# Attention branch's gate as Strassen-Winograd products behind the pooled branch, and weight sums by accumulating DMA, in a two-layer hybrid attention block

## The chip, the cores and the metric

One core of one Trainium2 chip runs the whole program. The metric is the device time in microseconds of one execution, lower is better. TensorE (PE) does the matrix products, VectorE (DVE), ScalarE (ACT) and GpSimd (POOL) the elementwise work, and DMAs are issued by SyncE (SP) and POOL.

## What is computed

Two layers run over T = 528 tokens (16 meta tokens and 512 of the input) of width 1024. In each layer, cut to what matters here:

```python
h = rms_norm(x, g)
q, k, v, gate_a, u_b, gate_b, q_idx, k_idx, w_idx, merge = split(h @ w_in)
attn = indexer_sparse_attention(...)      # 8 heads, top 128 keys by an indexer's score
y_a = (attn * silu(gate_a)) @ w_a         # gate_a: 512 columns of w_in, from column 640
y_b = (multiscale_pool(u_b) * silu(gate_b)) @ w_b
g_a, g_b = split(sigmoid(merge))          # merge: 2048 columns of w_in
x = x + (g_a * y_a + g_b * y_b) @ w_out
```

The result is float32. Each float32 product is three products of fp32r operands: high by high, high by low and low by high part (low = value minus its rounded copy).

## The kernel before

**Weights.** Every weight matrix is cut into chunks of 1 MB (`chunks`, L112). SP loads a chunk into two tiles `raw` (four buffers, so two chunks at a time), and a short list of steps then makes its high and low parts (`w`). `group_done` (L335) takes one step from the front of that list, `prep_q`, after a group of matmuls. There are three kinds of chunk. The ordinary kind (L188 onwards) has ACT round and DVE subtract. A chunk in `by_dma` (L202, L203, L207) has ACT write the negated rounded weights, an accumulating DMA from POOL's queue add the raw ones, and ACT round again. A chunk in `mixed` (`mixed_prep`, L227) makes seven operands out of four quarter blocks for seven products.

**Seven products instead of eight.** The merge gate's eight chunks go through `mix_gates` (L939): a chunk's 1024 by 256 weights and the activations are split into two by two blocks, and each gate (one chunk, q = 0 to 7) is seven block products (a11, a12, s2, s1, s3, s4, a22 in this order) of 12 matmuls each, 264 tokens wide in layer 0 and 256 in layer 1. Of the weights it needs four sums: s3 = a11 - a21, s2 = a22 - s3, s1 = a21 + a22, s4 = a12 - s2, all four made by DVE (`mix`, in steps i1, i2 and i4). Of a chunk's nine steps i0 to i8, each takes some high parts (ACT, L237) and low parts (DVE). The loop in `end` takes steps ahead of need: LEAD = 5 of the nine steps of the next gate are taken before that gate begins. The sums of the activations (`sums_of_h`, L867) are made while the pooled branch's gate and inputs are computed, some go out to DRAM and come back (`far`, `hsheet`), and from then on half of the normalized activations is overwritten by a sum, so no ordinary product of them may follow.

**Order of a layer.** Index queries and keys; gate_b (`silb`); the pooled branch's inputs u, with the pooling on POOL; `queries(0)` (half of the heads); gate_a as two `by_dma` chunks through `dense` (L547: 24 matmuls for one block of 128 columns and one stretch of tokens), with tanh on ACT (L1206) and a product on DVE into `sila`; `queries(1)`; then the product with w_b (16 blocks of 12 matmuls in layer 0, 8 wider ones in layer 1, `zb`, L1237); the eight gates; the product with w_a; the output.

**What runs beside it.** PE and DVE execute in the order in which the program text emits instructions (`manual_schedule`). Two streams are woven in. `fill` holds generators: first the indexer's scores (`index_steps`), then `attention` (L715), which is advanced by half of `rate[0]` turns per `half_done` (L329; a group_done counts as one). A head pair u (16 of them, in a loop of 18 rounds of three turns) goes through logits (PE), minimum (DVE), exp (ACT, L749), scaling (ACT, L760; POOL and DVE `pm`, L761), transposes (PE), copies (ACT, L776) and values (PE). Four head pairs share one block of 128 queries, and `gated(i)` (L802) multiplies a block's result into `sila`. In layer 0 six more turns treat the meta tokens. `attend` is put into `fill` before the product with w_b, at R_ATT = 1.95 and 1.7 for the two layers.

`sel` holds the top-k steps (`topk_steps`, L693): 16 rounds of MAX8 and MATCH_REPLACE8 on the scores, for two pairs of query blocks. `group_done` spends on them what an account has left: FULL times the estimated PE time since the last group, less the estimated DVE time (`pe_cost`, `dve_cost`, L81), at most CAP = 1.5 us. `ensure(i)` (L1213), called at the first logits of a query block, takes all steps that are still missing at once: the first pair's for blocks 0 and 1, the second pair's at block 2 (u = 8).

**Tiles.** `sheet` gives small tiles from six buffers ("tt") or wide ones from six buffers ("L", shared by the softmax rows `lt`, the sum s2 and others). All "d" products rotate through three PSUM banks.

Of the kernel before, what the change touches and what calls it, by code (L numbers as in the profile page):

```python
# [16 lines left out]
KT = D // 128  # L17
# [13 lines left out]
R_ATT = (1.95, 1.7)  # L31
FULL = 1.0
# [48 lines left out]
def dve_cost(name, out, a=None, *rest):  # L81
    if name == "memset":
        return 0.1
    n = max(cols(out), cols(a))
    return 0.15 + n * (0.00052 if name in ("tensor_copy", "tensor_scalar") else 0.00104)
# [3 lines left out]
def tile_block(ctx: ExitStack, tc: tile.TileContext, x, meta, w_in, pool_w, w_a, w_b, w_out, rows, hgain, c_tab, out):  # L89
# [24 lines left out]
    metas = {7: 0, 10: 1}  # L114
    for l in range(2):
        wi = w_rows(w_in[l], 0, w_in.shape[2])

        chunks.append([(wi[:, :, 2176:2432], 0)])
        plain.add(len(chunks))
        chunks.append([(wi[:, :, 512:640], 0), (wi[:, :, 2688:2816], 128)])  # L120
        mb = [3784, 4040, 4296, 4552]
        order = [2432, 1664, 1920, 1408, 1152, 0, 640, 896, 256]
        chunks += [[(wi[:, :, c:c + 256], 0)] for c in order]
        chunks += [[(w_rows(w_b[l], c, 512), 0)] for c in (0, 512)]
        by_dma |= set(range(len(chunks) - 10, len(chunks)))
        mixed |= set(range(len(chunks), len(chunks) + 8))
# [7 lines left out]
    def w_place():  # L134
        c = W["load"]
        W["load"] += 1
        kt = chunks[c][0][0].shape[1]
        raws[c] = [wpool.tile([128, kt // 2, 2048 // kt], F32, tag="raw", name="raw", bufs=4) for s in range(2)]
        return c

    def w_fetch(c, s):
        kt = chunks[c][0][0].shape[1]
        for src, o in chunks[c]:
            nc.sync.dma_start(raws[c][s][:, :, o:o + src.shape[2]], src[:, s * kt // 2:(s + 1) * kt // 2, :])
# [82 lines left out]
    def mixed_prep(c):  # L227

        r0, r1 = raws[c]
        blk = {"a11": r0[:, :, 0:128], "a21": r0[:, :, 128:256], "a12": r1[:, :, 0:128], "a22": r1[:, :, 128:256]}  # L230
        src = {"a11": "a11", "a12": "a12", "a22": "a22", "s3": "a11", "s2": "s2", "s1": "a21", "s4": "a12"}
# [10 lines left out]
        def mix(eng, to, x, y, op):  # L242
            eng.tensor_tensor(blk[to], blk[x], blk[y], op=op)

        def i0():
            hi("a11")

        def i1():
            lo("a11")
            mix(dve, "a11", "a11", "a21", OP.subtract)  # L250
            hi("a12")

        def i2():
            lo("a12")
            blk["s2"] = tmp.tile([128, 544], F32, tag="L", name="s2", bufs=LB)[:, :512].rearrange(
                "p (k e) -> p k e", k=4)
            mix(dve, "s2", "a22", "a11", OP.subtract)
            mix(dve, "a21", "a21", "a22", OP.add)
# [4 lines left out]
        def i4():  # L263
            lo("s2")
            mix(dve, "a12", "a12", "s2", OP.subtract)
# [449 lines left out]
    def attention(ensure):  # L715
# [92 lines left out]
        for u in range(-1, 17):  # L808
            if u + 1 < 16:
# [57 lines left out]
    def sums_of_h(l, s0, n2):  # L867
# [7 lines left out]
        def sums(g):  # L875
            k = slice(2 * g, 2 * g + 2)
            a0, a1, b0, b1 = nf[0][:, k, c0], nf[0][:, k, c1], nf[1][:, k, c0], nf[1][:, k, c1]
            dve.tensor_tensor(a0, a1, a0, op=OP.subtract)
            dve.tensor_tensor(a1, b1, a1, op=OP.subtract)
            dve.tensor_tensor(b1, b1, a0, op=OP.subtract)  # L880
# [4 lines left out]
        def lows(g):  # L885
            k = slice(2 * g, 2 * g + 2)
            a1, b0, b1 = nf[0][:, k, c1], nf[1][:, k, c0], nf[1][:, k, c1]
            dve.tensor_tensor(b0, b0, b1, op=OP.subtract)
# [6 lines left out]
        def fetch(w, g):  # L895
            if (w, g) == (0, 1):
                back[w, g] = [(slice(k, k + 1), sheet(n2, "hsheet")[:, None, :n2]) for k in (2, 3)]
            else:
                t = tmp.tile([128, T], F32, tag="B", name="hsheet", bufs=8) if w == 0 else sheet(T, "hsheet")
# [39 lines left out]
    def mix_gates(zb, ta, s0, n2, operands, splits, alos):  # L939
        base = popped[0] - progress[W["use"]]  # L940
        for q in range(8):
# [5 lines left out]
            U, S, X = (bs[r] for r in ROLES[q % 3])  # L947
# [11 lines left out]
            def end():  # L959
                done[0] += 1  # L960
                group_done()
                while prep_q and (popped[0] < base + 9 * q + LEAD + done[0] * 9 // 7 or (q == 7 and done[0] > 4)):
                    prep_one()

            def gate(eh, t, src, in_sheet):
                j = 2 * q + eh
                cs = slice(s0 + t * n2, s0 + (t + 1) * n2)
                if q < 4:
                    th = src if in_sheet else sheet(n2, "th")[:, :n2]
                    act.activation(th, src, AF.Tanh, scale=0.5)  # L970
                    d = zb[:, j, cs]
                    later(lambda: dve.scalar_tensor_tensor(d, th, 1.0, d, op0=OP.add, op1=OP.mult), 2)
                else:
                    act.activation(ta[j - KT][:, cs], src, AF.Tanh, scale=0.5)

            def total(eh, t, ps, part):
                o = sheet(n2, "c")[:, :n2]
# [35 lines left out]
            ready.pop(c)  # L1013

# [48 lines left out]
    for l in range(2):  # L1063
# [132 lines left out]
        queries(0)  # L1196
        sa = one.tile([128, 4, T], F32, tag="D", name="sila")
        SIL["a"] = sa
        for c in range(2):
            w = chunk()  # L1200
            for mi in range(2):
                j = 2 * c + mi
                for hf, a, n, o in halves:
                    ps = dense(w, mi, a, n)
                    th = sheet(n, "th")
                    act.activation(th[:, :n], ps[:, :n], AF.Tanh, scale=0.5)  # L1206
                    later(lambda th=th, ps=ps, j=j, a=a, n=n: dve.scalar_tensor_tensor(
                        sa[:, j, a:a + n], th[:, :n], 1.0, ps[:, :n], op0=OP.add, op1=OP.mult), 1)
                    group_done()
        queries(1)  # L1210
# [13 lines left out]
        fill.append(attend())  # L1224
        rate[0] = R_ATT[l]
# [16 lines left out]
        last_sum()  # L1242
        ahi = one.tile([128, 4, T], F32R, tag="Ahi", name="ahi")
# [14 lines left out]
        mix_gates(zb, ta, s0, n2, operands, splits, alos)  # L1258
# [154 lines left out]
```

## Time and profile before

| | |
|---|---|
| median of 3 runs | 757.07 us (756.95 to 758.25) |
| profiled execution | 756.37 us, of which its span is 754.6 us |
| granted PE clock | 1.00 |
| instructions | 15640 |
| DMA | 96.94 MB, 128 GB/s on average |
| accumulating DMAs of weights (POOL) | 40 of 512 KB |

A row of groups in the profile reads: line, engine, operation, tiles out<-in, shape, count, then busy time in us, mean ns of one, and the idle time of the engine ahead of it. L61 is a helper's line through which all of PE's and DVE's instructions go, so these are told by their tiles. The chain of work that ended last is printed in pieces that follow each other without overlap: start, duration, what.

### The profile page before, as it was taken

What the parts mean: (1) busy time and instruction counts of PE and PEld (TensorE: products, weight loads), DVE (VectorE), ACT (ScalarE), POOL (GpSimd) and SP (SyncE); (2) the same over time, 40 slices, a digit from 0 to 9 for tenths busy, and PEclk for the clock granted to TensorE, in tenths of its full rate; (3) what the DMA queues carried; (4) which work ended last, traced back from release to release, by engine and by line L of the source; (5) the groups of instructions that cost most, each with busy time, mean ns of one, the idle gap of its engine ahead of it and who ended that gap; (6) DMA issues with size and microseconds to landing.
All of it is one profiled execution on the core that took longest, in us unless ns stands there. A gap on an engine that the chain in (4) does not pass through costs nothing.

```text
span 754.6 us, 15640 instructions
## 1 busy us (share of the span) xinstructions
PE 739.7 (98%) x5914; PEld 707.6 (94%) x5914; DVE 563.7 (75%) x1416; ACT 471.8 (63%) x1049; POOL 213.8 (28%) x280
## 2 busy tenths in 40 slices
PE   8999999999989999999999999999999999999998
PEld 7999999999989999999999989988989899999998
DVE  6866987889798775894358668787998888678531
ACT  7679645558869795543245786555677788764320
POOL 3741075242012100063256401741501011005100
PEclk9999999999999999999999999999999999999999
DMA  7677757775122223543422787667812322146411
GB/s 263 226 167 173 166 127 179 158 200 139 31 82 57 57 57 96 184 143 127 128 87 83 171 190 186 157 151 203 208 38 61 98 67 56 57 135 204 140 43 43
DMA packets 73547, 96.94 MB, mean 128 GB/s; under 512 B 3664, under 2 KB 58736, under 8 KB 73472
## 3 DMA queue, kind: packets, MB, share of 16 engines
q1 hardware_dynamic: 67632, 74.89, 31.9%
q0 software_dynamic: 5760, 20.97, 14.8%
q8 instruction: 46, 0.75, 0.4%
q14 instruction: 29, 0.24, 0.1%
q10 hardware_dynamic: 80, 0.08, 0.0%
HBM read 66.41 MB, written 8.55 MB: 99 GB/s over the span
## 4 chain that ended last, share of the span: by engine, by line
PE 81%; DVE 9%; ACT 6%; issue 1%; POOL 1%; DMA 1%; SPq 0%; DVEq 0%; ACTq 0%
PE d L61 69%; PE a L61 10%; PE v L61 3%; DVE w L61 3%; ACT lt L749 2%; ACT w L237 1%; ACT lt L760 1%; DVE raw L61 1%; DVE lt L61 1%; ACT pt L776 1%; DVE c L61 1%; DVE s L61 1%; DVE sc L61 1%; DVE alo L61 1%; DMA xt<-in_x_dram 1%
## 5 line engine op out<-in xcount | busy, mean ns | idle before, releaser
L61 PE MATMUL d<-hhi,w 128*128 128x256 f32 (+3 forms) x1408 | 287.6, 296 | 0.3 <-DVE c L61 0.2
L61 PEld LDWEIGHTS d<-hhi,w 128*128 128x128 f32 x1408 | 225.9, 188 | 6.0 <-DVE c L61 0.7
L61 PE MATMUL d<-hlo,w 128*128 128x256 f32 (+3 forms) x704 | 193.5, 294 | 0.0
L61 PEld LDWEIGHTS d<-hlo,w 128*128 128x128 f32 x704 | 132.5, 188 | 2.6 <-issue 0.2
L61 PE MATMUL d<-w,hhi 128*128 128x256 f32 x768 | 121.0, 287 | 0.5 <-DVE w L61 0.5
L61 DVE TENSOR_TENSOR w<-raw,w 128x512 fp32r<-128x512 f32 (+1 forms) x128 | 107.7, 851 | 2.4 <-ACT w L237 2.3
L61 PEld LDWEIGHTS d<-w,hhi 128*128 128x128 f32 x768 | 104.3, 188 | 5.0 <-issue 2.1
L761 POOL TENSOR_SCALAR pm<-lt,rs 128x16 f32<-128x16 f32 x48 | 27.8, 592 | 173.3 <-DVE rs L61 166.4
L61 PE MATMUL d<-hsum,w 128*128 128x264 f32 (+1 forms) x576 | 76.6, 286 | 0.0
L61 PEld LDWEIGHTS d<-hsum,w 128*128 128x128 f32 x576 | 71.7, 188 | 0.7 <-ACT lt L760 0.3
L61 PE MATMUL d<-w,hlo 128*128 128x256 f32 x384 | 72.3, 281 | 0.0
L203 POOL DMA_DIRECT2D w<-raw x40 | 36.6, 929 | 104.4 <-ACT w L202 82.6
L237 ACT CAST w<-raw 128x512 fp32r<-128x512 f32 x96 | 56.9, 624 | 2.1 <-DVE raw L61 2.0
L61 PEld LDWEIGHTS d<-w,hlo 128*128 128x128 f32 x384 | 57.0, 188 | 0.0
L1274 POOL TENSOR_TENSOR hlo<-ta,hhi 128x256 fp32r<-128x256 f32 (+1 forms) x28 | 28.2, 1019 | 96.5 <-PE d L61 83.2
L61 DVE MATCH_REPLACE8 sc<-m,sc 128x400 f32<-128x400 f32 (+2 forms) x100 | 54.3, 548 | 0.0
L61 DVE MAX8 m<-sc 128x8 f32<-128x400 f32 (+2 forms) x100 | 52.7, 556 | 0.8
L749 ACT ACTIVATE lt<-lt,mn,NR 128x144 f32<-128x144 f32 (+3 forms) x64 | 42.4, 666 | 13.9 <-DVE mn L61 13.9
L61 PE MATMUL d<-mhi,w 128*128 128x272 f32 (+2 forms) x192 | 47.7, 328 | 0.0
L202 ACT ACTIVATE w<-raw 128x1024 fp32r<-128x1024 f32 x40 | 41.4, 1057 | 8.3 <-PE d L61 8.3
L61 DVE SCALAR_TENSOR_TENSOR sc<-r,wsg,sc 128x144 f32<-128x144 f32 (+3 forms) x56 | 32.3, 580 | 16.2 <-ACT r L673 14.1
L207 ACT CAST w<-raw 128x1024 fp32r<-128x1024 f32 x40 | 41.5, 1050 | 0.0
(209 smaller groups left out, 1391.2 us busy)
## 6 DMA issues: line engine op xcount, KB each, us to landing
raw<-in_w_in_dram SPq DMA_DIRECT2D x72, 512.0 KB, 4.1
w<-raw POOLq DMA_DIRECT2D x40, 512.0 KB, 5.3
raw<-in_w_out_dram SPq DMA_DIRECT2D x16, 512.0 KB, 3.4
kept<-res SPq DMA_DIRECT2D x16, 264.0 KB, 4.0
res<-kept SPq DMA_DIRECT2D x16, 264.0 KB, 5.8
raw<-in_w_branch_b_dram SPq DMA_DIRECT2D x8, 512.0 KB, 3.8
raw<-in_w_branch_a_dram SPq DMA_DIRECT2D x8, 512.0 KB, 3.7
xt<-in_x_dram SPq DMA_DIRECT2D x4, 512.0 KB, 5.6
```

Of the source, the lines that this page charges most:

```text
L61: return fn(*a, **k)
L202: act.activation(t, raws[c][s], AF.Copy, scale=-1.0)
L203: gp.dma_start(t, raws[c][s], accum_op=OP.add)
L207: act.copy(t, raws[c][s])
L237: act.copy(t[:, 0], blk[src[n]])
L749: act.activation(L[hh][:, :n], L[hh][:, :n], AF.Exp, scale=NR[:, i, h:h + 1], bias=mn[:, hh:hh + 1], accum_out=sm[:, hh:hh + 1])
L760: act.activation(L[hh][:, 16:n], L[hh][:, 16:n], AF.Copy, scale=rs[:, hh:hh + 1])
L761: (gp if j < 3 else dve).tensor_scalar(pms[i][:, 2 * j + hh, :], L[hh][:, 0:16], rs[:, hh:hh + 1], None, op0=OP.mult)
L776: act.copy(pt[:, :2 * len(bs)], tp[:, :256 * len(bs)].rearrange("p (a c) -> p a c", c=128))
L1274: pool_end = gp.tensor_sub(hlo[:, j, a:a + n], d, f(hhi[:, j, a:a + n]))
```

## The change

- gate_a's two chunks (columns 640 and 896) move behind the pooled branch's chunks, become `mixed`, and run through `mix_gates` as q = -2 and -1, ahead of the merge gate's eight. `queries(1)` follows `queries(0)` directly.
- `sila` is then written by these two gates. `attend` enters `fill` after the product with w_b, and `attention` yields without work at u = 4 until four groups after gate -1 has ended (`SIL["ready"]`).
- The sums of weights become s3 = a11 + a21, s2 = s3 + a22, s1 = a21 + a22, s4 = a12 + s2. DVE makes s3 and s2, and an accumulating DMA from POOL's queue makes s1 and s4. Signs move into the sums of activations, and into tanh's scale.
- A mixed chunk's quarter blocks are contiguous in `raw`; it is loaded by four DMAs of 256 KB instead of two of 512 KB.
- R_ATT becomes (1.75, 1.6), FULL 1.05, and `dve_cost` a smaller fixed part.
- The returned sum `hsheet` (0, 0) takes a wide "L" tile instead of a "B" tile.

The diff, cut to its core:

```diff
-R_ATT = (1.95, 1.7)
-FULL = 1.0
+R_ATT = (1.75, 1.6)
+FULL = 1.05
...
-    return 0.15 + n * (0.00052 if name in ("tensor_copy", "tensor_scalar") else 0.00104)
+    each = 0.00052 if name in ("tensor_copy", "tensor_scalar") else 0.00104
+    return {"match_replace": 0.13, "tensor_tensor_reduce": 0.18}.get(name, 0.07) + n * each
...
-        order = [2432, 1664, 1920, 1408, 1152, 0, 640, 896, 256]
+        order = [2432, 1664, 1920, 1408, 1152, 0, 256]
...
-        chunks += [[(wi[:, :, c:c + 256], 0)] for c in (*mb, 2760, 3016, 3272, 3528)]
+        chunks += [[(wi[:, :, c:c + 256], 0)] for c in (640, 896, *mb, 2760, 3016, 3272, 3528)]
...
+            for eh in range(2):
+                nc.sync.dma_start(raws[c][s][:, eh], src[:, 4 * s:4 * s + 4, eh * 128:eh * 128 + 128])
...
         def i0():
+            blk["s3"] = tmp.tile([128, 544], F32, tag="L", name="s3", bufs=LB)[:, :512].rearrange(
+                "p (k e) -> p k e", k=4)
+            dve.tensor_add(blk["s3"], blk["a11"], blk["a21"])
+            gp.dma_start(blk["a21"], blk["a22"], accum_op=OP.add)
             hi("a11")
         def i1():
             lo("a11")
-            mix(dve, "a11", "a11", "a21", OP.subtract)
+            dve.tensor_add(blk["a11"], blk["s3"], blk["a22"])
             hi("a12")
         def i2():
             lo("a12")
-            blk["s2"] = tmp.tile([128, 544], F32, tag="L", name="s2", bufs=LB)[:, :512].rearrange(
-                "p (k e) -> p k e", k=4)
-            mix(dve, "s2", "a22", "a11", OP.subtract)
-            mix(dve, "a21", "a21", "a22", OP.add)
+            gp.dma_start(blk["a12"], blk["a11"], accum_op=OP.add)
...
         def i4():
             lo("s2")
-            mix(dve, "a12", "a12", "s2", OP.subtract)
             hi("s1")
...
         for u in range(-1, 17):
+            while u == 4 and not SIL["ready"]:
+                yield
...
-        for q in range(8):
+        for q in range(-2, 8):
...
+                sign = -1.0 if eh else 1.0
+                if q < 0:
+                    th = sheet(n2, "th")[:, :n2]
+                    act.activation(th, src, AF.Tanh, scale=0.5)
+                    d = sa[:, j + 4, cs]
+                    later(lambda: dve.scalar_tensor_tensor(d, th, sign, src, op0=OP.add, op1=OP.mult),
+                          3 if in_sheet else 2)
...
+            if q == -1:
+                later(lambda: SIL.update(ready=True), 4)
...
         queries(0)
+        queries(1)
         sa = one.tile([128, 4, T], F32, tag="D", name="sila")
-        for c in range(2):
-            w = chunk()
-            for mi in range(2):
-                j = 2 * c + mi
-                for hf, a, n, o in halves:
-                    ps = dense(w, mi, a, n)
...
-        queries(1)
...
-        fill.append(attend())
-        rate[0] = R_ATT[l]
...
         last_sum()
+        fill.append(attend())
+        rate[0] = R_ATT[l]
```

More of the change, by code (lines that the diff above doesn't have):

```diff
@@ L137, in w_place @@
         kt = chunks[c][0][0].shape[1]
-        raws[c] = [wpool.tile([128, kt // 2, 2048 // kt], F32, tag="raw", name="raw", bufs=4) for s in range(2)]
+        shape = [128, 2, 4, 128] if c in mixed else [128, kt // 2, 2048 // kt]
+        raws[c] = [wpool.tile(shape, F32, tag="raw", name="raw", bufs=4) for s in range(2)]
         return c
```

49 lines of the change are left out of this document (23 added, 26 removed).

## The prediction

> **What bounds the kernel now.** The page's head comes first, then its first and second part, for the engine that is never free and for its clock.
>
> ```profile
> span 754.6 us, 15640 instructions
> PE 739.7 (98%) x5914; PEld 707.6 (94%) x5914; DVE 563.7 (75%) x1416; ACT 471.8 (63%) x1049; POOL 213.8 (28%) x280
> PEclk9999999999999999999999999999999999999999
> ```
>
> PE is busy in 739.7 of 754.6 us at the full granted clock, so the time is the sum of the matmuls plus 14.9 us in which PE stands. What a change is worth is the matmul time that it takes away plus what it does to those 14.9 us. Where they lie, the windows by stage tell: gate_a in layer 0, the product with w_b, then three windows of the eight gates, and the same gates in layer 1 (columns: length; busy time and count of PE, PEld, DVE, ACT, POOL; clock; DMA share; GB/s).
>
> ```profile
> 128.70:153.90 25.20, 25.20 (x213) 25.00 (x210) 22.04 (x60) 15.45 (x28) 8.78 (x10) 1.00 0.57 126
> 167.30:196.30 29.00, 29.00 (x246) 28.84 (x245) 26.10 (x86) 24.86 (x70) 7.96 (x15) 1.00 0.41 108
> 196.30:230.00 33.70, 31.73 (x279) 30.70 (x278) 31.15 (x85) 25.09 (x63) 4.05 (x6) 1.00 0.23 64
> 230.00:270.00 40.00, 38.88 (x336) 37.50 (x335) 31.77 (x90) 34.51 (x82) 5.35 (x8) 1.00 0.21 55
> 270.00:311.00 41.00, 40.42 (x363) 39.17 (x363) 28.47 (x62) 27.53 (x65) 0.98 (x2) 1.00 0.29 87
> 566.00:600.00 34.00, 32.95 (x285) 31.76 (x286) 29.11 (x81) 27.29 (x70) 4.03 (x6) 1.00 0.25 65
> 600.00:640.00 40.00, 39.47 (x354) 38.05 (x351) 32.88 (x89) 32.78 (x78) 6.22 (x9) 1.00 0.27 78
> 640.00:678.00 38.00, 37.25 (x340) 35.88 (x339) 27.23 (x63) 27.39 (x60) 2.32 (x4) 1.00 0.27 86
> ```
>
> Up to the gates PE never stands. In the gates it stands 1.97 + 1.12 + 0.58 = 3.7 us in layer 0 and 1.05 + 0.53 + 0.75 = 2.3 us in layer 1, 6.0 us together; the rest lies in stages that the change leaves alone. The waits of each gate stage and DVE's order of time say what most of the 6.0 us is.
>
> ```profile
> PEld a L61 <- ACT lt L760: 2.8, 3, 2.1
> ```
>
> ```profile
> 217.41 1.18 DVE L61 MAX8 m<-sc 128x8 f32<-128x400 f32 x2
> 219.11 0.69 DVE L61 MATCH_REPLACE8 sc<-m,sc 128x528 f32<-128x528 f32 x1
> 219.72 0.70 DVE L61 TENSOR_SCALAR sc<-sc 128x400 f32<-128x400 f32 x2
> ```
>
> ```profile
> 591.57 1.85 DVE sc L61 x4
> ```
>
> ```profile
> PEld a L61 <- ACT lt L760: 2.1, 4, 1.1
> ```
>
> Here `ensure` takes the rest of the second pair's top-k at once, a whole round (2.3 us from the first MAX8 to the TENSOR_SCALAR) and the ends, 3.0 us of DVE in these rows. The reciprocal behind it is late, then ACT's scaling, then PE's transposes: the one wait of 2.1 us. In layer 1 the piece of 1.85 us in the chain, from 591.57, does the same, for 1.1 us. So 3.2 of the 6.0 us are forced top-k; 2.8 us are short waits of the attention.
>
> **The change part by part.**
>
> *Columns of matmul (the main term).* In the chain of work, whose pieces follow each other without overlap, a gate_a block of 24 matmuls takes this in layer 0 at 272 and at 256 columns, and one in layer 1 at 512; behind them stand two long stretches of the gates, at 264 and 256 columns.
>
> ```profile
> 129.00 3.06 PE d L61 x24
> 132.93 2.90 PE d L61 x24
> 502.38 2.86 PE d L61 x12
> 297.23 13.36 PE d L61 x108
> 666.46 8.71 PE d L61 x72
> ```
>
> The piece of 2.86 us has only 12 matmuls, half a block, so layer 1's four blocks are eight such pieces. Before: 4 x (3.06 + 2.90) = 23.8 us and 8 x 2.86 = 22.9 us. After, two gates of 84 matmuls in each layer: 168 x 13.36/108 = 20.8 us and 168 x 8.71/72 = 20.3 us. The difference is 3.0 + 2.6 = **-5.6 us**, the eighth that seven products save, less a little since short matmuls cost more for each column. PE has no cover here and nothing to wait for in gate_a now, so all of it counts.
>
> *Work of DVE and ACT.* The rows of one low part, one sum, one high part, one total and gate_a's product (one row of its source line stands for its tanh):
>
> ```profile
> L61 DVE TENSOR_TENSOR w<-raw,w 128x512 fp32r<-128x512 f32 x96 | 64.8, 683 | 2.4 <-ACT w L237 2.3
> L61 DVE TENSOR_TENSOR raw<-raw 128x512 f32<-128x512 f32 x32 | 22.0, 687 | 0.6
> L237 ACT CAST w<-raw 128x512 fp32r<-128x512 f32 x96 | 56.9, 624 | 2.1 <-DVE raw L61 2.0
> L61 DVE TENSOR_TENSOR c<-d,p 128x264 f32<-128x264 f32 x16 | 6.8, 428 | 10.3 <-PE d L61 6.9 <-ACT lt L749 1.8 <-ACT lt L760 1.5
> L1206 ACT ACTIVATE th<-d x12: 374/398/598, 133.0 to 526.0; 128x272 f32<-128x272 f32 x4, 128x256 f32<-128x256 f32 x4, 128x512 f32<-128x512 f32 x4
> ```
>
> A chunk costs DVE 11 x 0.68 us before and 9 x 0.68 after. In layer 0 the gates' windows hold 91.4 us of DVE in 114.7. After: less 8 x 2 x 0.68 = 10.9, plus two chunks 12.3, plus 14 totals and gates at 0.43 = 6.0, plus the five rounds of attention that now lie beside w_b (about 7 us, my estimate from that window's 26.1 less top-k), less the 4 us of top-k left: about 102 us in 114.7 + 20.8 = 135.5 us, 75% instead of 80%. ACT gets 14 x 0.62 + 14 x 0.4 + about 8 = 22 us on 87.1, so 81% instead of 76%. Both stay beside PE: cost 0, between -2.8 us (all short waits go) and +2 (they grow with ACT's share). The changed sums of activations keep their count and sizes; 0.
>
> *Top-k.* DVE's groups in the 26 us ahead of w_b and in w_b's own window, two MAX8 to a round:
>
> ```profile
> L61 DVE MAX8 m<-sc 128x8 f32<-128x528 f32 (+1 forms) x13 | 7.8, 634 | 0.0
> ```
>
> ```profile
> L61 DVE MAX8 m<-sc 128x8 f32<-128x400 f32 (+1 forms) x12 | 7.0, 628 | 0.0
> ```
>
> w_b now comes 25 us earlier, so some 14 rounds instead of 7 are open at its start, at 2.3 us of DVE each. But w_b's window loses the attention, about 19 of its 23 us of DVE become free, and the new account takes more: two MAX8 of 400 and 528 columns took 1.18 us, the old formula puts 1.27, the new one 1.11, and FULL adds 5%. DVE was 22.04 of 25.20 in gate_a's window, and the slack of 12% there and ahead goes to top-k. By u = 8, four gates on, I expect little left to force. Of 3.2 us I take **-2.5** (0 to -3.2). A denser DVE can also be late for PE in the query stages, where q_post reads PSUM: I take **+0.5**, between 0 and 4, the one credit of 1.5 us and 5% of some 50 us.
>
> *Two sums by DMA.* The nearest rows are the accumulating DMAs of twice the size, and the loads with the new short rows beside the old ones.
>
> ```profile
> L203 POOL DMA_DIRECT2D w<-raw x40: 849/874/1218, 43.6 to 540.0; - x40
> DMA to landing us min/median/max: 4.4/5.3/9.4
> raw<-in_w_in_dram SPq DMA_DIRECT2D x72, 512.0 KB, 4.1
> raw<-in_w_in_dram SPq DMA_DIRECT2D x8, 256.0 KB, 4.6
> ```
>
> POOL issues 72 in place of 40, at 0.87 us: 28 us on an engine that is busy in 10.4 of 114.7 us of the gates. Behind a DMA that waits for DVE only `pm` is queued, and its readers come at the end of a query block. The additions are awaited by ACT: s1 is issued in i0 and rounded in i4, s4 issued in i2 and rounded in i6, each time three products apart. A gate lasts 114.7/8 = 14.3 us, so three products are 6.1 us. A landing of 5.3 us after issue fits, with 0.8 us for DVE's lag and for a `pm` ahead of it. If it is late, ACT stands in the cast with exps and copies queued behind it, and PE waits for those. I take **+1.0**, from 0 to 11 (below). [...] The loads: 4.6 instead of 4.1 us, a gate ahead of use and twice as many issues on SP, which PE never awaits; 0.
>
> *Attention's end.* A product gives half of R_ATT: 0.875 and 0.8 turns instead of 0.975 and 0.85. Attention needs 18 x 3 turns, 60 with the meta tokens: 60/0.875 = 69 of the 70 products in layer 0, 54/0.8 = 68 in layer 1. SIL is ready at product 18, when 15.75 and 14.4 turns have been given and 15 are used before u = 4, so hardly a turn is wasted. But now the last `gated`, its split and low part come right ahead of w_a. Before, in layer 0, they ended some ten products earlier:
>
> ```profile
> L61 PE MATMUL v<-pt,VM x4: 217/241/265, 296.9 to 297.0; 16*64 16x64 f32 x4
> ```
>
> ```profile
> L61 PE MATMUL d<-ahi,w x256: 277/281/384, 315.2 to 701.6; 128*128 128x256 f32 x96, 128*128 128x272 f32 x32
> ```
>
> The meta tokens' values, the last of the attention, stand at 297 us, and w_a begins at 315. DVE 0.68, ACT 0.62, DVE 0.69 us in a row, most of it under the last two products and the first block of w_a: **+1.0** for both layers (0 to 5).
>
> Sum: -5.6 - 2.5 + 0.5 + 1.0 + 1.0 = -5.6 us. The profiled execution took 756.37 us, 1.8 around its span and 0.7 below the median of the runs: 750.8, as a median **751.5 us**.
>
> **The rivals.**
>
> *Late additions (slower).* If the DMAs land at 7.4 us, halfway from 5.3 to 9.4, each cast waits 1.2 us: 40 x 1.2 = 48 us of ACT standing. With a quarter of that on PE, 12 us in place of the 1.0: 762. For it: ACT at 81%, POOL in order, 9.4 seen. Against: half the bytes, DMA share of 0.21 to 0.29 in the gates. It decides from (5.6 + 1.0)/40 = 0.17 us of PE wait for each DMA on. [...]
>
> *Attention comes late.* Turns that find DVE or ACT behind push its end past the last gate, into `drain`, where PE has nothing else: at the upper 5 us in place of 1.0, and the forced top-k kept whole, 751.5 + 4 + 2.5 = 758.0, about no change; half of it, 754.8.
>
> *All waits go.* With the 2.8 us of short waits and 3.2 of top-k gone, and no new ones: 757.1 - 5.6 - 6.0 = 745.5; half way 748.
>
> *The columns don't shrink.* If boundaries between short products ate the gain, 757. The two stretches quoted are whole products with their boundaries; hardly.
>
> **How the numbers follow.** The forecast (748.5 to 755.5) gets 0.56, fewer waits 0.13, late attention 0.15, late additions 0.15, no shrinking 0.01. A measurement of this kernel can tell about 0.2%, 1.5 us. Faster: 0.56 + 0.13 + half of late attention = 0.76; same: 0.08; slower: late additions and a rest, 0.16. The range runs from 746.5, which leaves 0.03 below, to 758.5, with the late additions above.
>
> **What would show it.** Right: 168 instead of 192 and 96 matmuls on gate_a's weights, PE's busy time down by 5 to 6 us; no wait of 2 us ahead of the transposes of u = 8, MAX8 ended before them; casts L237 with little idle time behind DMA `raw`; the meta tokens' matmuls just ahead of w_a. Wrong: ACT's casts waiting for the additions, above 0.5 us each; PE idle before w_a by several us; new waits in the queries and in w_b for DVE.

## The result and the profile after

The changed kernel takes **764.17 us** (median of 5 runs, 762.57 to 765.64) beside 758.25 us for the kernel before (5 runs, 756.95 to 758.96). The ratio is **1.008**, 95% interval 1.0057 to 1.0102: slower by 0.8%, where 751.5 us was forecast. Every ratio below is to the kernel before as it ran beside the kernel named, with its 95% interval in brackets; 0.01 is 7.6 us. The profiled execution of the kernel after took 762.6 us.

The head of the page and its row of engines:

```profile
span 760.7 us, 15982 instructions
PE 738.2 (97%) x5962; PEld 708.9 (93%) x5962; DVE 569.7 (75%) x1436; ACT 474.9 (62%) x1077; POOL 238.4 (31%) x312
```

PE is busy for 1.5 us less than before instead of 5 to 6, and it stands for 22.5 us instead of 14.9. The windows by stage say where: in layer 0 the end of the queries, w_b (145.0 to 170.6) and the ten gates; in layer 1 w_b (520.0 to 543.4) and the first gates. The columns are those of the prediction's table.

```profile
130.00:145.00 15.00, 14.73 (x132) 13.52 (x125) 14.32 (x42) 10.04 (x22) 10.04 (x12) 1.00 0.89 213
145.00:170.60 25.60, 25.47 (x213) 25.14 (x212) 25.50 (x65) 15.77 (x37) 8.09 (x9) 1.00 0.55 135
170.60:210.00 39.40, 35.83 (x293) 34.21 (x292) 35.52 (x104) 26.90 (x75) 6.05 (x12) 1.00 0.46 107
210.00:250.00 40.00, 36.40 (x303) 34.92 (x302) 30.43 (x86) 31.30 (x78) 9.50 (x14) 1.00 0.45 103
250.00:290.00 40.00, 38.64 (x354) 37.67 (x355) 26.86 (x77) 32.48 (x76) 7.97 (x13) 1.00 0.46 110
290.00:320.20 30.20, 29.66 (x264) 28.64 (x260) 20.43 (x46) 20.53 (x46) 2.56 (x3) 1.00 0.44 115
520.00:543.40 23.40, 23.40 (x112) 19.02 (x111) 23.30 (x60) 13.21 (x24) 6.51 (x8) 1.00 0.55 128
543.40:580.00 36.60, 33.61 (x261) 32.47 (x260) 33.09 (x96) 24.80 (x69) 6.59 (x11) 0.95 0.47 109
```

Two things are new. DVE has hardly any time free from 130 us to the end of w_b (14.32 of 15.00, 25.50 of 25.60, and 23.30 of 23.40 in layer 1), where the prediction counted on DVE time becoming free. And in the gates PE stands for 3.57 + 3.60 + 1.36 + 0.54 = 9.1 us in layer 0 (3.7 before) and for 3.0 us in the first stretch of layer 1's gates, with the clock at 0.95 there. The waits between 140 and 320 us name the second half of the story.

```profile
ACT w L244 <- DMA raw<-raw: 11.4, 10, 3.7
PEld d L61 <- ACT p L997: 4.9, 3, 3.0
PE d L61 <- ACT p L997: 4.3, 3, 2.8
PE d L61 <- DVE w L61: 1.5, 1, 1.5
```

ACT's rounding of s1 and s4 (L244) stands ten times for the accumulating DMA, up to 3.7 us at once. `p` (L997) is ACT's copy of a product out of PSUM, which is queued behind that rounding, and PE's next product waits for it. The timeline shows one such case, row by row (in brackets the idle time ahead of it and its releaser; `s` is the sum s3):

```profile
230.42 2.19 ACT L244 CAST w<-raw 128x512 fp32r<-128x512 f32 x4 [0.62 <-DMA raw<-raw]
...
236.16 0.67 DVE L61 TENSOR_TENSOR s<-raw 128x512 f32<-128x512 f32 x1
236.23 13.04 SPq L148 DMA_DIRECT2D raw<-in_w_in_dram  x4
...
236.44 1.44 POOL L765 TENSOR_SCALAR pm<-lt,rs 128x16 f32<-128x16 f32 x2 [8.42 <-DVE rs L61]
...
237.82 0.89 POOL L253 DMA_DIRECT2D raw<-raw  x1
...
242.83 0.62 ACT L244 CAST w<-raw 128x512 fp32r<-128x512 f32 x1 [3.68 <-DMA raw<-raw]
...
246.04 0.28 PE L61 MATMUL d<-hhi,w 128*128 128x264 f32 x1
...
248.66 0.38 ACT L997 COPY p<-d 128x264 f32<-128x264 f32 x1
...
249.09 1.52 PEld L61 LDWEIGHTS d<-hsum,w 128*128 128x128 f32 x12 [2.98 <-ACT p L997]
```

The third of the four casts in the first row rounds a11, in step i0, at 231.4. DVE makes s3, of the same step, only at 236.16, and POOL issues s1's addition behind that and behind a `pm`, at 237.82. ACT is at the cast of s1 by 239.15, 1.3 us after the issue. The addition lands at 242.80, 4.98 us after the issue. ACT has lost 3.68 us by then and comes to `p` only at 248.66, and PE stands for 2.8 us behind its matmul of 246.04. The group of all 40 additions shows neither the late issue nor the late landing, because its median is 3.2 us:

```profile
raw<-raw POOLq DMA_DIRECT2D x40, 256.0 KB, 3.2
```

### The profile page after: what moved, and what is told of

The parts are those of the page before. It is cut to its first block, busy times and chain, and to the rows that moved or that the text cites. A ratio compares the mean times of both kernels' runs of the same rounds, so it can differ in the third digit from the quotient of the medians.

```text
span 760.7 us, 15982 instructions
## 1 busy us (share of the span) xinstructions
PE 738.2 (97%) x5962; PEld 708.9 (93%) x5962; DVE 569.7 (75%) x1436; ACT 474.9 (62%) x1077; POOL 238.4 (31%) x312
## 4 chain that ended last, share of the span: by engine, by line
PE 62%; DVE 19%; ACT 9%; DMA 6%; issue 3%; POOL 1%; DVEq 0%; SPq 0%; ACTq 0%; POOLq 0%
PE d L61 52%; PE a L61 8%; DMA raw<-raw 5%; DVE sc L61 4%; DVE m L61 3%; DVE w L61 3%; ACT w L244 3%; ACT lt L753 2%; DVE t L61 2%; PE v L61 2%; DVE qs L61 1%; ACT lt L764 1%; DVE ss L61 1%; DMA xt<-in_x_dram 1%; ACT pt L780 1%
## 5 line engine op out<-in xcount | busy, mean ns | idle before, releaser
L61 PE MATMUL d<-hhi,w 128*128 128x256 f32 (+3 forms) x1344 | 268.8, 292 | 0.5 <-DVE sila L61 0.3
L61 PEld LDWEIGHTS d<-hhi,w 128*128 128x128 f32 x1344 | 214.8, 189 | 3.8 <-issue 0.6
L61 PE MATMUL d<-hlo,w 128*128 128x256 f32 (+3 forms) x672 | 183.2, 289 | 0.0
L61 DVE TENSOR_TENSOR w<-raw,w 128x512 fp32r<-128x512 f32 (+1 forms) x152 | 124.5, 829 | 4.0 <-ACT w L244 3.9
L61 PE MATMUL d<-hsum,w 128*128 128x264 f32 (+1 forms) x720 | 98.5, 289 | 7.8 <-ACT p L997 4.5
L61 PEld LDWEIGHTS d<-hsum,w 128*128 128x128 f32 x720 | 91.0, 191 | 10.4 <-ACT p L997 5.7
L244 ACT CAST w<-raw 128x512 fp32r<-128x512 f32 x120 | 70.8, 620 | 40.8 <-DVE raw L61 20.9
L210 POOL DMA_DIRECT2D w<-raw x32 | 29.5, 940 | 72.5 <-ACT w L209 50.0
L61 DVE SCALAR_TENSOR_TENSOR sc<-r,wsg,sc 128x144 f32<-128x144 f32 (+3 forms) x56 | 32.3, 581 | 16.1 <-ACT r L677 13.6
L253 POOL DMA_DIRECT2D raw<-raw x20 | 17.8, 889 | 79.3 <-DVE s L61 74.9
L640 POOL TENSOR_TENSOR t<-t,t 128x256 f32<-128x256 f32 (+1 forms) x34 | 30.8, 907 | 26.8 <-DVE t L61 26.5
```

The costliest lines, as they stand in the source:

```text
L61: return fn(*a, **k)
L210: gp.dma_start(t, raws[c][s], accum_op=OP.add)
L244: act.copy(t[:, 0], blk[src[n]])
L253: gp.dma_start(blk["a21"], blk["a22"], accum_op=OP.add)
L640: gp.tensor_tensor(t1[:m, :256], t1[:m, :256], t2[:m, :256], op=OP.add)
```

## The experiments

Theory 1 at the start: the additions by DMA land too late for ACT. Theory 2: DVE, crowded by top-k behind w_b, is late for PE. Rivals: the attention's place and rates; the new account; the seven products do not shrink gate_a.

### Who pays: the two sums

**a_dve_sums**: the kernel after, s1 and s4 added by DVE.

```diff
         def i0():
...
-            gp.dma_start(blk["a21"], blk["a22"], accum_op=OP.add)
...
         def i2():
             lo("a12")
-            gp.dma_start(blk["a12"], blk["a11"], accum_op=OP.add)
+            dve.tensor_add(blk["a21"], blk["a21"], blk["a22"])
...
         def i4():
             lo("s2")
+            dve.tensor_add(blk["a12"], blk["a12"], blk["a11"])
```

> The changed kernel with s1 and s4 added by DVE (two additions of 0.68 us more for each of 20 chunks, none by DMA). Theory 1, late additions: ACT's casts no longer wait for a DMA (19.3 us in 17 waits in the changed kernel), so neither does PE for ACT's copy p (about 5 us of PE in layer 0); the time falls by about 5 us against the changed kernel, to about 759. Theory 2, top-k too dense: DVE is full from 130 to 210 us anyway and gets 27 us more work, so the time stays near 764 or rises by 1 to 3.

Measured: 755.2 us, 0.9974 [0.9963, 0.9986], better than theory 1 expected. The additions by DMA cost 1.06 points, **8 us**, more than DVE's 40 extra additions do.

**e_late_casts**: the additions stay with the DMA, but the results are rounded one step later (s1 in i5, s4 in i7; s3 and a22 go ahead; NEEDS 6 and 8).

```diff
         def i4():
             lo("s2")
-            hi("s1")
+            hi("s3")
         def i5():
-            lo("s1")
-            hi("s3")
+            lo("s3")
+            hi("s1")
...
```

> The changed kernel with the same work, but the casts of s1 and s4 come one step later (s3 and a22 are rounded first), about 1.6 us more from addition to cast. Theory 1: most of the 17 waits of ACT for a DMA (mean 1.1 us) go, and PE's waits for p and the exps with them: about 760. Theory 2: PE's waits come from DVE's backlog, and it stays at 764 within 1 us.

Measured: 757.58 us, 1.0002 [0.9992, 1.0013]: 0.78 points, 6 us, from the order of the casts alone. ACT now stands for the additions 10 times for 9.3 us in all, instead of 17 times for 19.3.

**i_s4_by_dma**: s1 by DVE (in i4), s4 by DMA, both rounded late as in e.

```diff
         def i0():
...
-            gp.dma_start(blk["a21"], blk["a22"], accum_op=OP.add)
...
         def i4():
             lo("s2")
-            hi("s1")
+            dve.tensor_add(blk["a21"], blk["a21"], blk["a22"])
+            hi("s3")
...
```

> The changed kernel with s1 by DVE, s4 alone by DMA, and with the later casts. Of the 17 waits of ACT for a DMA 11 were for s1, the long ones among them, and those that remain with the later casts were 6. Theory 1: no wait over 1 us remains, DVE saves 0.68 us a chunk against sums all by DVE: 753.5 to 755.5. If any addition by DMA costs (POOL's issue, the DMA engines), 756 or more.

Measured: 753.9 us, 0.9958 [0.9943, 0.9973], 0.44 points under e. So with the late casts it is s1's addition by DMA that costs, and s4's costs nothing that shows beside a; 11 of the 17 casts that stood in the kernel after were s1's.

### The account, and the attention's rates

**b_old_account** is the kernel after with FULL = 1.0 and the old `dve_cost`; **c_sums_account** is b with a's sums.

```diff
-FULL = 1.05
+FULL = 1.0
...
-        return 0.08
+        return 0.1
...
-    return {"match_replace": 0.13, "tensor_tensor_reduce": 0.18}.get(name, 0.07) + n * each
+    return 0.15 + n * each
```

> The changed kernel with FULL = 1.0 and the old dve_cost, so that top-k is spread as thinly as before. Theory 2, top-k too dense: DVE is no longer full ahead of the first gates, its additions and low parts are on time there, and the waits of the first 40 us of gates (3.6 us of PE in layer 0, 3.0 in layer 1, and a dip of the clock of 1.7 us) go: about 759. Theory 1, late additions: the waits at 187, 246 and 260 us stay, and more top-k is forced at u = 8 (2 to 3 us for each layer): 763 to 768.

> The changed kernel with s1 and s4 added by DVE and the old account of top-k: of the change only gate_a as fourteen products, the new sums' signs and the rates are left. If theories 1 and 2 each hold a part, this is the fastest of the four: the columns' 5.6 us less against before, so 753 to 755. If the placement itself is at fault (attention beside ten gates, its end at w_a), it stays at 758 or above.

Measured: b 782.96 us, 1.0342 [1.0322, 1.0361]; c 780.75 us, 1.0315 [1.0293, 1.0338]. b lies far above both times expected of it, and c far above the 758 that was to speak against the placement. Without the new account the move would have cost 3.4%. A row of b's waits and two of its windows:

```profile
PE d L61 <- DVE w L61: 13.6, 1, 13.6
```

```profile
200.00:228.40 28.40, 24.38 (x200) 23.20 (x199) 22.91 (x62) 21.73 (x56) 7.22 (x10) 1.00 0.44 99
228.40:245.50 17.10, 5.34 (x24) 5.34 (x25) 16.02 (x47) 3.79 (x11) 0.00 (x0) 0.50 0.12 31
```

At u = 8 the rest of top-k is forced on DVE, PE waits 13.6 us for a low part `w` behind it, and then runs at half the clock for what is left of 17.1 us.

**f_before_account** is the reverse: the kernel before with only FULL = 1.05 and the new `dve_cost`.

```diff
-FULL = 1.0
+FULL = 1.05
...
-        return 0.1
+        return 0.08
...
-    return 0.15 + n * (0.00052 if name in ("tensor_copy", "tensor_scalar") else 0.00104)
+    each = 0.00052 if name in ("tensor_copy", "tensor_scalar") else 0.00104
+    return {"match_replace": 0.13, "tensor_tensor_reduce": 0.18}.get(name, 0.07) + n * each
```

> The kernel before with the new account of top-k alone (FULL = 1.05, new dve_cost). Theory P, the placement of gate_a in the gates gains its columns: this kernel only loses the forced top-k at u = 8 (3.2 us of PE) and stays above the changed kernel with DVE's sums (755.2): 755 to 757. Theory Q, the placement gains nothing and the account made the whole gain of that kernel: 754 or less.

Measured: 753.36 us, 0.9953 [0.9937, 0.9969]. Its windows of gate_a and of the gate stretch in which the kernel before stood for 2 us:

```profile
128.70:153.90 25.20, 25.20 (x213) 25.03 (x212) 25.10 (x69) 15.46 (x30) 8.39 (x9) 1.00 0.57 126
196.00:230.00 34.00, 34.00 (x302) 33.37 (x300) 29.34 (x78) 27.90 (x72) 4.06 (x6) 1.00 0.23 63
```

DVE takes 25.10 us of top-k and other work beside gate_a instead of 22.04, and nothing is left to force: PE is busy in 34.00 of 34.00. In the kernel before the account is worth 0.47 points by itself; 3 us more of DVE's work lie under gate_a's 25 us.

**h_dve_sums_old_rates** is a with the rates of before.

```diff
-R_ATT = (1.75, 1.6)
+R_ATT = (1.95, 1.7)
```

> The changed kernel with sums by DVE, and with R_ATT = (1.95, 1.7) as before. Attention would end 7 products earlier in layer 0, so the wait ahead of w_a (0.8 and 0.4 us) goes, but it then reaches u = 4 before gate_a's sums are ready (18 products give 17.5 turns, 2.5 of them without work in layer 0) and is denser beside the gates. If the low rate is worth something: 756 to 758; if attention's late end is the dearer: 754.

Measured: 754.85 us, 0.9968 [0.9955, 0.9982], beside a's 0.9974: the rates do nothing that can be told.

### The parts without the move

**g_before_dma_sums** is the kernel before with the new sums, signs and loads, gate_a dense and the old account; **k_all_but_gates** adds the new account, so it is all of the change but gate_a's move, its rates and `SIL`; **n_all_but_gates_late** is k with e's late casts. Against the kernel after, k is

```diff
-        order = [2432, 1664, 1920, 1408, 1152, 0, 256]
+        order = [2432, 1664, 1920, 1408, 1152, 0, 640, 896, 256]
...
-        for q in range(-2, 8):
+        for q in range(8):
```

with gate_a dense between the two `queries`, and R_ATT as before.

> The kernel before with the new sums alone: s1 and s4 by DMA, blocks contiguous, signs moved; gate_a stays in its old place. Theory 1, late additions: 16 chunks and 32 additions instead of 40 cost about 0.8 of what they cost in the changed kernel (9 us), so 762 to 766. If additions are late only because DVE is full of top-k in the changed kernel, they are in time here: 755 to 758.

> The kernel before with the new sums by DMA and the new account: all of the change but gate_a's move into the gates and the rates that go with it. Theory R, the move takes 25 us of PE time away from ahead of attention, so top-k, which has to end there, fills DVE and runs on into the first gates, and DVE's, POOL's and ACT's lateness costs more than the columns: this kernel is the fastest so far, 751 to 754, about 11 us below the changed one. Theory 1 alone, additions by DMA cost wherever DVE is dense: 757 or more.

> All of the change but gate_a's move, and the casts of s1 and s4 one step later. With the additions beside ordinary gates ACT waited 13.3 us for them in 14 waits; these should mostly go. As PE waited little there, 1 to 2 us below the same kernel with the casts in the old order; if PE's short waits in the gates come from DVE and attention alone, no difference.

Measured: g 757.1 us, 0.9991 [0.9979, 1.0004]; k 755.92 us, 0.9972 [0.9956, 0.9987]; n 754.23 us, **0.9931 [0.9915, 0.9947]**. With eight gates and gate_a ahead, the DMAs cost nothing beside the DVE sums that they replace, and with the new account 0.2 points (k beside f), which is not clear of noise; k lies between the two times expected of it. ACT's casts stand for the additions there too, 14 times for 13.2 us in k, but PE waits for `p` for only 0.2 us; why it pays so little there stays open. The late casts take 0.4 points off k (n). n beats both kernels. The kernel after is 1.08 points slower than k, so in this setting the move itself costs 8 us instead of saving 5.6.

### Room on DVE

In these three only 8 of the 16 rounds of top-k are run, so half of the selection is left out.

```diff
-        for rnd in range(16):
+        for rnd in range(8):
```

**o_dve_sums_8_rounds** is a with that edit, **l_after_8_rounds** the kernel after, **m_all_but_gates_8_rounds** is k.

> The changed kernel with sums by DVE and 8 rounds of top-k instead of 16 (half of the selection left out): gate_a's move with neither late additions nor a full DVE. The column term as predicted (5.6 us) would put it at 748 to 750, about 5 us below the kernel before with the new account (753.4, which has no forced top-k either). If the short products save less, or two more gates bring waits of their own: 751 to 754.

> The changed kernel with 8 rounds of top-k instead of 16 (it selects 64 keys, so half of the selection is left out: some 27 us of DVE less in each layer). Theory R: DVE has room ahead of the gates, the additions are issued in time, and most of 13 us of waits and the dip of the clock go: 750 to 753. Theory 1 alone: additions come late in the later gates as before (waits at 246 and 260 us): 758 or more.

> All of the change but gate_a's move, with 8 rounds of top-k instead of 16 (half of the selection left out). It has no forced top-k to lose, so by theory R it stays within 1 us of the same kernel with 16 rounds. The difference to the changed kernel with 8 rounds is then what the move is worth where DVE has room: by the column term 4 to 5.6 us in favour of the move; near 0 if the short products don't save what the rows promised.

Measured: o 745.79 us, **0.9841 [0.9825, 0.9856]**; l 756.8 us, 0.9989 [0.9973, 1.0005]; m 756.26 us, 0.9974 [0.9963, 0.9985]. m equals k, so with gate_a in its old place half of top-k is worth nothing: it is covered. o is 1.33 points, 10 us, faster than a: behind the move it isn't covered. l lies between the two times expected of it, and o below both of its own. First o's page, then its windows of w_b and of the first gates, then the same two of a:

```profile
PE 735.3 (99%) x5962; PEld 708.6 (95%) x5962; DVE 543.2 (73%) x1332; ACT 474.2 (64%) x1077; POOL 206.2 (28%) x272
```

```profile
146.30:171.30 25.00, 25.00 (x210) 24.84 (x209) 10.28 (x20) 15.23 (x36) 6.71 (x7) 1.00 0.51 127
171.30:210.00 38.70, 38.54 (x320) 37.44 (x319) 34.21 (x96) 30.12 (x85) 4.65 (x8) 1.00 0.32 83
210.00:250.00 40.00, 40.00 (x351) 39.38 (x350) 33.41 (x90) 33.60 (x83) 6.08 (x10) 1.00 0.30 80
```

```profile
144.70:170.00 25.30, 25.17 (x209) 24.83 (x208) 25.20 (x64) 14.42 (x33) 6.17 (x7) 1.00 0.50 126
170.00:210.00 40.00, 38.38 (x313) 36.75 (x312) 38.55 (x109) 29.23 (x82) 3.10 (x8) 1.00 0.31 80
210.00:250.00 40.00, 37.38 (x314) 36.46 (x313) 35.72 (x96) 33.04 (x83) 4.88 (x8) 1.00 0.26 67
```

With room on DVE (10.28 of 25.00 in w_b) PE stands for 0.2 us in the first 79 us of the gates; in a, with DVE at 25.20 of 25.30 and then 38.55 of 40.00, it stands for 4.2 us in 80. Over the whole span PE stands for 16.6 us in a and for 10.0 us in o. The last of the rows for MAX8 gives the time of the last round, 584 us in a's layer 1 (542 in f):

```profile
L61 DVE MAX8 m<-sc x100: 299/566/697, 81.1 to 584.1; 128x8 f32<-128x272 f32 x32, 128x8 f32<-128x400 f32 x32, 128x8 f32<-128x528 f32 x32, 128x8 f32<-128x144 f32 x4
```

o is also 1.12 points, 8.5 us, under f, and its PE is busy 4.3 us less and stands 2.2 us less: the columns saved are there. l shows the other half by itself. It has room on DVE and is still 1.48 points, 11 us, slower than o. Its waits and one window:

```profile
ACT w L244 <- DMA raw<-raw: 11.7, 9, 3.9
...
PE d L61 <- ACT p L997: 5.9, 2, 3.0
```

```profile
210.00:250.00 40.00, 33.81 (x264) 32.75 (x263) 26.17 (x72) 31.33 (x80) 7.58 (x12) 0.93 0.40 93
```

Two waits of 3 us behind late additions, and a clock of 0.93. So crowding and late additions are two costs; neither needs the other. Taken in the other order, the DMAs cost 1.48 points with room on DVE (o to l), and the full DVE costs 0.91 on top of them (l to after).

### Why an addition lands late

In the kernel after, 12 of the 40 additions take over 3.7 us, and ahead of ten of these SP issued a load 0.8 to 1.6 us earlier. Five runs tried to move the load behind s1. **p_loads_later** emits it in i3 of the next chunk instead of i8 of its own; **r_both_later** is p with e's casts; **q_no_gates_late_loads** is n with p's edit.

```diff
         def i8():
             lo("a22")
             del raws[c]
-            w_load()
+            if c + 1 in mixed:
+                held.append(c)
...
```

> The changed kernel with the load of the next mixed chunk three steps later, so that it no longer starts just ahead of the addition for s1. If that load is what makes s1 land in 4.7 to 5.4 us instead of 3.2, the long waits of ACT (2.6 to 3.9 us) and the PE waits at 246 and 260 us go: 757 to 760. If the lateness comes from DVE's and POOL's order alone, 764 as the changed kernel.

> The whole change with later casts and later loads: additions by DMA without lateness, DVE as full of top-k as in the changed kernel. 753 to 755, as with sums by DVE less some microseconds of DVE; if the addition that stayed late with the later casts (3.2 us of ACT, 2.95 of PE, a dip of the clock) is due to something other than the load, 757 as there.

> All of the change but gate_a's move, with the later casts and the later loads. A candidate for the fastest: 0 to 1.5 us below the same kernel without the later loads (ratio 0.993 to before), so 750.5 to 752.5 where before takes 757.

Measured: p 763.13 us, 1.0067 [1.0052, 1.0081]; r 758.08 us, 1.0004 [0.999, 1.0017]; q 753 us, 0.9944 [0.9921, 0.9967]. **s_load_after_s1** and **t_late_casts_and_loads** emit the load right behind the cast of s1, in the kernel after and in n.

```diff
-            act.copy(t[:, 0], blk[src[n]])
+            cast = act.copy(t[:, 0], blk[src[n]])
+            if n == "s1" and held:
+                held.pop()
+                with tc.issue_after(cast.ins):
+                    w_load()
...
```

> The kernel after, with one edit: while the gates run, SP issues the load of a later chunk only after ACT has rounded s1, so that no load's packets are under way when the addition of s1 starts. The load then has about half a gate, some 7 us, until its chunk is needed and takes 4 to 5 us. If the additions come late because a load runs ahead of them, s1 lands 3.2 us after its issue instead of 4.7 to 5.4, the waits of 3 to 4 us of ACT at its cast and the two PE waits behind them go, and the time is 757 to 761. If the landing is not what the time hangs on (DVE's lag alone), the time stays at 764.

> The fastest version so far (all of the change but gate_a's move and the attention's rates, the cast of the sums one step later; 0.9931 of before), with the load of a later chunk issued only after ACT has rounded s1, a product later than in the run above. If loads ahead of the additions still cost something there, 751 to 753 beside a time before of 758; if the later casts had already hidden the additions, no change, 0.993 of before; slower than that if a load is now late for its chunk.

Measured: s 763.0 us, 1.0062 [1.0044, 1.008]; t 754.35 us, 0.995 [0.993, 0.997]. None of the five tells anything about the load, because none moved it. In p SP's issues for these loads run from 141.1 to 649.8 us (L148), in the kernel after from 139.2 to 648.3. What they wait for is not a place in the text: in the kernel after the waits of L148 ended 16 times with the landing of an addition (142.6 us in all) and 20 times with DVE's low part `w` (63.1 us). In s the load at 235.65 us still went out 1.6 us ahead of the addition at 237.24, which landed after 5.1 us; why the edit did not hold it back stays open. The test that the expectations describe was not made. The five do tell how well a ratio repeats: p and s lie at 1.0067 and 1.0062 beside the kernel after at 1.0080, r at 1.0004 beside e at 1.0002, and q and t at 0.9944 and 0.995 beside n at 0.9931.

The traces say more than these runs. The 14 kernels with additions by DMA hold 492 of them, and I sorted them by two things: whether SP issued a load between 2 us before and 0.9 us after POOL's issue, and whether an instruction fetch (a packet of the kind `instruction`, 16 KB on queue 8 or mostly 8 KB on queue 14) ran on a DMA engine between 1.4 and 3.2 us after it.

| | additions | landing, us: median (min to max) | over 3.7 us |
|---|---|---|---|
| neither | 245 | 3.22 (3.15 to 3.91) | 2 |
| a load | 106 | 3.85 (3.16 to 6.87) | 70 |
| a fetch | 66 | 3.55 (3.18 to 5.19) | 28 |
| both | 75 | 5.02 (3.20 to 5.97) | 64 |

In the kernel after alone the four groups hold 19, 9, 4 and 8 additions, and 0, 3, 2 and 7 of them took over 3.7 us. Its DMA view shows the addition of 237.82 from inside. Columns are packets, MB and the share of 16 engines; first from 239.2 to 240.8 us, then from 240.8 to 242.2.

```profile
q0 software_dynamic: 135, 0.25, 84.7%
q8 instruction: 1, 0.02, 6.7%
q1 hardware_dynamic: 29, 0.01, 2.6%
```

```profile
q0 software_dynamic: 7, 0.01, 7.3%
```

The load (q1) is nearly done when the addition (q0) begins. One fetch, a single packet from 239.38 to 241.09 us, takes 6.7% of 16 x 1.6 us, 1.7 us. In the next 1.4 us seven packets of the addition start, from 241.07 on, 0.16 to 0.21 us apart, and nothing else does. The landing, at 242.80, comes only behind them. That they stood behind the fetch on its engine is read from these times; the view does not name the engines.

With a load and a fetch at once an addition took 5.0 us at the median, with neither 3.2. That loads and fetches are the cause of the late landings is read from these counts; no run moved either.

The late landing is only half of why a cast stands. In the kernel after all 40 additions landed within 5.35 us of their issue, but ACT was at the cast 3.6 us after the issue at the median (1.3 to 7.9), and less than 5.3 us after it in 34 of 40. Had every addition landed in 3.2 us, ACT would by the same times still have stood for 9.5 of its 19 us (an estimate from the issue, landing and cast times of the 40). The other half is the late issue: s1's follows DVE's s3 by 0.3 to 1.0 us, and comes 4.8 us (median of 20) after ACT's cast of a11, which stands in the same step i0. DVE comes to that step later than ACT. In e, a step later, ACT is at the cast of s1 5.3 us after the issue at the median, instead of 3.7.

## Why the prediction was wrong

In points of the ratio, from runs of complete parts (each step's interval is some 0.2 points to either side):

| step | from, to | points | us |
|---|---|---|---|
| account, gate_a in its place | before, f | -0.47 | -3.6 |
| the move, with room on DVE | f, o | -1.12 | -8.5 |
| the move, DVE full | o, a | +1.33 | +10.1 |
| s1, s4 by DMA | a, after | +1.06 | +8.0 |
| sum | | +0.80 | +6.1 |

**Columns of matmul (-5.6).** Right in kind: 8.5 us (6 to 11 by the intervals) between f and o, of which PE's busy time explains 4.3; o also leaves out half of top-k, which m shows to be worth nothing without the move. PE's count rose by 48, which is 2 x 168 - 288 as worked out, and the rival in which the columns don't shrink falls. In the kernel after the gain is there and is eaten by the two steps below.

**Top-k (-2.5 + 0.5) and DVE's work (0): this step failed first.** That by u = 8 little would be left to force came true: the last round ran at 199 us in layer 0 and at 565 us in layer 1, and the longest wait of PE ahead of the transposes is 1.4 us instead of 2.1. The account does what was expected of it where gate_a still lies ahead of the attention (f: -3.6). What failed is the price of DVE's lateness for PE in the gates: 0, from a mean of 75% over ten gates and with all of top-k taken out of them, and 0.5 for the query stages alone. The prediction's own count did not fit that. It had 14 rounds of 2.3 us still to come when w_b begins, 32 us, and 19 us of DVE to become free there. In the kernel after it was 22 MAX8 in layer 0 and 20 in layer 1, 11 and 10 rounds; about 19 and 18 us of top-k filled w_b's window (25.50 of 25.60 us busy), and about 10 and 9 us went on into the first gates, where PE awaits DVE's low parts and totals.

```profile
L61 DVE MAX8 m<-sc x100: 298/567/698, 81.6 to 565.4; 128x8 f32<-128x272 f32 x32, 128x8 f32<-128x400 f32 x32, 128x8 f32<-128x528 f32 x32, 128x8 f32<-128x144 f32 x4
```

The last round in the kernel after, at 565.4 us, stands 22 us behind the start of layer 1's gates at 543.3. The first gates decided and not the mean: +10 us (o to a) where -2.0 was forecast.

**Two sums by DMA (+1.0, range 0 to 11): this step failed too.** The mechanism was named, as the rival with late additions at 762, and given 0.15; it measures +8.0, in the range but not at the value taken. The landing that the step took, 5.3 us, was enough: the latest of the 40 took 5.35, the median 3.2. What failed is the room. The step took the distance in the program's text, three products or 6.1 us from issue to cast, with 0.8 us for DVE's lag and a `pm`. Measured it is 3.6 us at the median. For s1 the reason is DVE's lag behind ACT: its sum and with it the issue come 4.8 us after ACT's cast of the same step. That the total of 762 lies near the measured time is in part luck: the rival reached it with landings of 7.4 us, which never came, and the +10 us of the full DVE are not in it. POOL's issues took about the 0.87 us that the step put for each: those of s1's additions 0.85 to 0.91 us, and those of s4's 0.85 to 1.01 us.

```profile
L253 POOL DMA_DIRECT2D raw<-raw x20: 852/893/912, 164.4 to 666.2; - x20
```

**A quarter of ACT's standing on PE.** Now 19.3 us of standing casts in 17 waits cost 8 us, so the pass-through was nearer to four tenths, partly by the clock (below). In k it was next to nothing, so it is no constant.

**Attention's end (+1.0).** Right. PE waits for `ahi` 0.6 us ahead of w_a in layer 0, and in layer 1 for a low part `w` 0.2 us.

```profile
PE d L61 <- ACT ahi L1255: 0.6, 1, 0.6
```

The rivals *attention comes late* and *all waits go* are out: h shows that the rates don't matter, and behind the last gate PE stands for no more than these 0.8 us ahead of w_a.

Two sums among the rivals are off by half a microsecond, without weight for the forecast: halfway between 745.5 and 751.5 is 748.5, and 12 us in place of 1.0 gives 762.5.

## What to carry to other kernels

Before work is moved off a stage, ask what was hidden under it and where that goes: here 25 us of dense product were the cover of top-k, and without them the saved columns were paid back by DVE. The room of a transfer is counted from when the engines ahead of its issue get there, and not from its place in the text (here 3.6 us at the median and not 6.1); the cheap remedy is order, and rounding the result one step later was worth 6 us. Small parts are worth running alone: the account and the sums with late casts, without the move, have the lowest ratio of all complete versions, 0.9931 [0.9915, 0.9947] of the kernel before, and 0.9944 and 0.995 in q and t, which repeat it. The account alone, at 0.9953 [0.9937, 0.9969], is not clearly behind.

## What the runs showed of the hardware

**The clock.** After some stretches of 3.4 us in which PE stood for about half of the time or more it was granted half the clock for the next 3.4 us; in b, for 17.1. Three windows of the kernel after, and two of e:

```profile
558.50:561.90 3.40, 3.38 (x29) 3.23 (x29) 2.30 (x7) 2.11 (x7) 0.09 (x1) 1.00 0.45 78
561.90:565.30 3.40, 1.74 (x13) 1.19 (x11) 3.37 (x12) 3.12 (x8) 0.53 (x2) 1.00 0.55 151
565.30:568.70 3.40, 3.40 (x16) 3.40 (x17) 1.81 (x5) 1.73 (x7) 0.89 (x1) 0.50 0.68 173
```

```profile
244.10:247.50 3.40, 1.13 (x9) 1.13 (x10) 2.94 (x9) 3.40 (x9) 0.00 (x0) 1.00 0.00 0
247.50:250.90 3.40, 3.40 (x19) 3.40 (x18) 1.37 (x4) 2.72 (x8) 0.00 (x0) 0.50 0.59 154
```

In the kernel after, two waits of 1.2 and 0.45 us with matmuls between them were enough: PE was busy in 1.74 of 3.40 us. At half the clock a dip costs up to half of its 3.4 us, 1.7 (an estimate). Yet the wait of 2.8 us behind 246.04 in the kernel after brought none, while two waits of about the same length in l, 5.9 us together, did. In l each lay within one stretch: PE was busy for 0.58 of 3.40 us (210.1 to 213.5) and for 0.56 of 3.40 (244.3 to 247.7), and the clock in the next 3.4 us was 0.51 and 0.50. In the kernel after the wait was shared by two stretches, in which PE was busy for 1.92 of 3.50 us (244.4 to 247.9) and 2.21 of 3.40 (247.9 to 251.3), and the clock stayed at 1.00. So the length of a wait did not tell by itself whether a dip followed. In the trace of the kernel after the clock fell at 565.292 us and came back at 568.706, 3.413 us later; it fell again at 759.852, behind another 191.146 us, 56 times 3.4133. Nor does a busy share tell it by itself: 1.74 of 3.40 us was followed by a dip there, and in the kernel before 1.61 of 3.40 (749.6 to 753.0) was not, where PE had no matmul left to run in the next stretch. What the clock goes by, no run shows.

**Fetches.** The fetch of 16 KB at 239.4 us in the kernel after took 1.7 us, and the addition that it ran beside landed 4.98 us after its issue, 1.8 us behind the median of all 40. That this one packet set when the addition had landed is read from the times above; no run shows it.
